# A decoder trunk on one core: S5 local matrices read from memory by overlapping transfers, two K units moved forward, the first block in another order

## The chip, the cores and the metric

One core of one Trainium2 chip. A core has TensorE (PE, matrix products and transposes), VectorE (DVE), ScalarE (ACT), GpSimd (POOL) and SyncE (SP, which issues transfers); each takes its instructions in a written order and waits on semaphores. The metric is the device time of one execution in microseconds (us), median of the runs. "TensorE's pass" below is one matmul instruction.

## The reference

```python
mem_n = _rmsnorm(mem, mem_norm)                       # 256 memory tokens
for i in range(2):                                    # x is (1, 256, 1024)
    g = norm_gains[i]
    x = x + 0.5 * _swiglu(_rmsnorm(x, g[0]), ffn1_w_in[i], ffn1_w_out[i])     # 1024 -> 2 x 2816 -> 1024
    h = _rmsnorm(x, g[1])
    mix = _s5_mixer(h, ...) if i == 0 else _retention_mixer(h, positions, ...)
    x = x + mix
    x = x + _memory_cross_attention(_rmsnorm(x, g[2]), mem_n, w_q[i], w_kv[i], w_o[i])
    x = x + 0.5 * _swiglu(_rmsnorm(x, g[3]), ffn2_w_in[i], ffn2_w_out[i])
return _rmsnorm(x, final_norm)
```

The S5 mixer runs, for each of 64 groups of 16 channels, a diagonal complex state of 64: state = a * state + B u, y = Re(C state) + d * u, then gelu, then a gated product with `w_glu`. The cross attention takes K and V from `mem_n @ w_kv`; they do not depend on x.

## The kernel before

Everything is float32. A product by a weight is made of three matmuls, since a weight tile is split into a rounded part `wh` and a rest `wl`, and the activations likewise (`xTh`, `xTl`): wh by high, wl by high, wh by low. The 256 tokens are two halves of 128 (tt 0 and 1).

**Weight stream** (class `Stream`). A plan, written once, lists all tiles of 512 KB in the order of use. `pump` sends the next load on SP's queue as soon as one of five raw buffers is free (the tile `raw`); ACT makes `wh` (line 86), DVE subtracts to make `wl` (line 88), which frees the raw buffer; seven pairs of `wh`/`wl` exist. Tiles that are tables (fourth field False) are used from the raw buffer itself, and free it only at `ws.done`. SP sends in order: where the next load waits for its buffer, everything behind it on SP waits too. `hold` and `release` put subtractions off and let them go (line 105).

**S5 by chunks of eight steps.** The tokens are regrouped to 32 chunks of 8 steps: after the norm, `S5In.stat(tt)` writes `xn` to memory (`xn_d`) and reads it back in another order (`xc`), half 0 on POOL's queue, half 1 on SP's. `s5` then copies xc to `xg`, transposes it (`U`), multiplies by the V tables (input to state, `v<-...,U`), turns the result to `S`, and runs the scan over 31 chunks on DVE in small steps (`adv`). Beside the scan TensorE makes the part of y that lies inside a chunk: for each of eight q a table of 128 x 1024, the local matrices (a kernel of eight taps, shifted once for each output step), multiplies U. The function `local_table` makes that table: POOL copies the taps into a row of 15 blocks padded by zeros (`pad`), TensorE transposes eight overlapping windows of it, ACT copies the result to `L`. After the scan the C tables (`carry`) add the state's part, then `gelu`, then `y_out` turns y and splits it for the gate product (`yT`). V tables 2 and 3 and C tables 0 to 3 are loaded to tiles of their own (`ytab`, and the unused ends of `kvh`/`kvl`); V and C tables 4 to 7 pass through raw buffers. The tables were computed earlier, by the background list `bg` during the first ffn, and stored by POOL.

**Filler.** Where S5 leaves TensorE idle, `fill(us)` takes steps of the K and V units of layer 0's cross attention: units 0 to 3 are K (8 steps of 6 passes of 256 columns), units 4 and 5 V (8 steps of 6 passes of 512). Layer 1's units are computed after the retention mixer.

**Background list.** `bg_step` runs one yield's worth of `s5_tables` (called `tabs`) or of `mem_steps` (norm and transposes of the memory tokens) at set places of the ffn; `bg_flush` runs what is left, just ahead of the residual add.

**First block.** The order of the first ffn block is written by hand: `turned` transposes x, `high` and `low` make `xTh` and `xTl`, `part(tt, c, ...)` multiplies by weight tile c ("hh" is wh by high, "hl" wl by high, "lh" wh by low), `spin(n)` multiplies a scratch tile n times to keep TensorE running, `next(tabs)` takes a step of the S5 tables, `n0.stat` sums the squares of x on ACT.

## Time and profile before

| | |
|---|---|
| median of 3 runs | 1282.44 us (1281.72 to 1284.2) |
| profiled execution | 1278.4 us, its span 1276.6 us |
| TensorE | busy 1255.8 us (98%), granted clock 0.996 |
| DVE, ACT, POOL | 821.1, 630.0 and 61.4 us |
| memory traffic | 242.05 MB, mean 190 GB/s |

A waits row reads: engine, output, line, what it waited for, total time, times. Busy time of TensorE includes the tails of passes that overlap the next, so the start-to-start distance is the price of a pass. In a windows row the columns are the window, its length, then busy time and count of PE, weight loads, DVE, ACT and POOL, the granted clock, the busy share of the transfer engines, and GB/s.

### The profile page before, as it was taken

The numbers are of one execution on the slowest core, as the hardware profiler recorded it, in microseconds if no ns is written. First come the engines' busy times: TensorE is split into PE (matmuls) and PEld (weight loads), VectorE is DVE, ScalarE is ACT, GpSimd is POOL, SyncE is SP. The second block draws the span as 40 slices with busy tenths as digits, with TensorE's granted clock in tenths as the row PEclk, the third lists the DMA queues.
The fourth block names the chain that finished last, engine by engine and source line by source line (L and its number), as shares of the span: only waits on it lengthen the run. The fifth ranks groups of instructions, "written<-read, shape, count | busy, mean of one in ns | idle before, by whom it ended". The sixth has DMA issues, their size and how long they took to land.

```text
span 1276.6 us, 18149 instructions
## 1 busy us (share of the span) xinstructions
PE 1255.8 (98%) x6884; PEld 1056.3 (83%) x6884; DVE 821.1 (64%) x1142; ACT 630.0 (49%) x849; POOL 61.4 (5%) x116
## 2 busy tenths in 40 slices
PE   8999999898999999999999999999999999999997
PEld 5778888877898888888888888899888898888886
DVE  5989986496667755645655546677665646755543
ACT  5645545455455644444545435544544545644532
POOL 4010001000000000001000000001100000000000
PEclk9999999999999999999999999999999999999999
DMA  7856786655645656664765664653674734766560
GB/s 225 239 182 220 251 272 212 216 199 184 207 155 182 210 181 187 207 189 140 243 190 181 197 191 138 218 186 104 215 233 141 231 103 128 235 198 186 188 188 33
DMA packets 166008, 242.05 MB, mean 190 GB/s; under 512 B 10641, under 2 KB 130049, under 8 KB 165281
## 3 DMA queue, kind: packets, MB, share of 16 engines
q1 hardware_dynamic: 161856, 226.80, 56.4%
q0 software_dynamic: 3552, 13.28, 3.3%
q8 instruction: 54, 0.88, 0.3%
q10 hardware_dynamic: 512, 0.82, 0.2%
q14 instruction: 34, 0.27, 0.1%
HBM read 229.32 MB, written 11.53 MB: 189 GB/s over the span
## 4 chain that ended last, share of the span: by engine, by line
PE 80%; DMA 1%; ACT 1%; issue 0%; DVE 0%; POOL 0%; POOLq 0%; ACTq 0%; DVEq 0%; SPq 0%
PE acc L241 61%; PE kv L241 6%; PE pt L245 4%; PE qk L241 4%; PE q L241 2%; PE s L241 1%; PE o L241 1%; PE y L249 1%; PE rv L241 1%; DMA xn_d<-xn 0%; PE rs L241 0%; DMA raw<-in_xattn_w_kv 0%; DMA xc<-xn_d 0%; PE v L249 0%; ACT yT L328 0%
## 5 line engine op out<-in xcount | busy, mean ns | idle before, releaser
L88 DVE TENSOR_TENSOR wl<-raw,wh 128x1024 fp32r<-128x1024 f32 x404 | 489.3, 1225 | 199.0 <-ACT wh L86 186.9
L86 ACT CAST wh<-raw 128x1024 fp32r<-128x1024 f32 x408 | 423.5, 1051 | 180.7 <-PE acc L241 150.7
L241 PE MATMUL acc<-wh,xTh 128*128 128x512 f32 x864 | 326.3, 398 | 0.2 <-ACT wh L86 0.2
L241 PE MATMUL acc<-wl,xTh 128*128 128x512 f32 x864 | 319.5, 390 | 2.1 <-DVE wl L105 2.1
L241 PE MATMUL acc<-wh,xTl 128*128 128x512 f32 x864 | 320.6, 392 | 0.0
L241 PEld LDWEIGHTS acc<-wl,xTh 128*128 128x128 f32 x864 | 162.5, 188 | 35.2 <-DVE wl L105 2.9
L241 PEld LDWEIGHTS acc<-wh,xTl 128*128 128x128 f32 x864 | 162.3, 188 | 34.8 <-DVE xTl L1342 0.7
L241 PEld LDWEIGHTS acc<-wh,xTh 128*128 128x128 f32 x864 | 162.7, 189 | 34.1 <-ACT wh L86 1.5
L241 PE MATMUL acc<-wh,hTh 128*128 128x512 f32 x352 | 138.7, 394 | 0.0
L241 PE MATMUL acc<-wh,hTl 128*128 128x512 f32 x352 | 137.2, 390 | 0.0
L241 PE MATMUL acc<-wl,hTh 128*128 128x512 f32 x352 | 137.1, 389 | 0.0
L468 ACT ACTIVATE s<-acc,rstd 128x256 f32<-128x256 f32 x88 | 41.8, 474 | 152.0 <-PE acc L241 149.2
L470 DVE SCALAR_TENSOR_TENSOR h<-acc,rstd,s 128x256 f32<-128x256 f32 x88 | 42.3, 480 | 90.9 <-ACT s L468 90.8
L241 PEld LDWEIGHTS acc<-wh,hTl 128*128 128x128 f32 x352 | 66.1, 188 | 14.0
L241 PEld LDWEIGHTS acc<-wh,hTh 128*128 128x128 f32 x352 | 66.1, 188 | 13.9 <-issue 0.6
L241 PEld LDWEIGHTS acc<-wl,hTh 128*128 128x128 f32 x352 | 66.1, 188 | 13.2
L289 ACT ACTIVATE junk<-x 128x512 bf16<-128x512 f32 (+1 forms) x27 | 20.9, 772 | 72.5 <-DVE x L368 70.5
L368 DVE SCALAR_TENSOR_TENSOR x<-acc,x 128x512 f32<-128x512 f32 x28 | 18.5, 686 | 39.1 <-PE acc L241 39.1
L280 POOL TENSOR_SCALAR ms<-ss 128x1 f32<-128x1 f32 x11 | 2.6, 239 | 825.0 <-ACT junk L289 824.9
L241 PE MATMUL acc<-wh,yT 128*128 128x512 f32 x128 | 39.1, 400 | 2.6 <-ACT yT L328 2.4
L241 PE MATMUL acc<-wh,ryT 128*128 128x512 f32 x128 | 40.1, 390 | 0.0
L241 PE MATMUL kv<-memh,wh 128*128 128x256 f32 x128 | 37.0, 289 | 0.0
(297 smaller groups left out, 1611.0 us busy)
## 6 DMA issues: line engine op xcount, KB each, us to landing
raw<-in_ffn_w_in SPq DMA_DIRECT2D x352, 256.0 KB, 4.3
raw<-in_ffn_w_out SPq DMA_DIRECT2D x88, 512.0 KB, 4.3
raw<-in_ret_w_in SPq DMA_DIRECT2D x48, 512.0 KB, 4.4
raw<-in_xattn_w_kv SPq DMA_DIRECT2D x32, 512.0 KB, 4.7
raw<-in_s_w_glu SPq DMA_DIRECT2D x32, 256.0 KB, 4.3
raw<-in_xattn_w_q SPq DMA_DIRECT2D x16, 512.0 KB, 4.9
raw<-in_xattn_w_o SPq DMA_DIRECT2D x16, 512.0 KB, 3.9
raw<-in_ret_w_out SPq DMA_DIRECT2D x16, 512.0 KB, 4.4
```

Source lines behind the costliest of these rows:

```text
L86: self.nc.scalar.copy(hi, raw)
L88: self.nc.vector.tensor_sub(lo, raw, hi.bitcast(F32))
L241: pe.matmul(o, lhsT=a, rhs=b, start=start, stop=stop)
L245: pe.transpose(o, a, i)
L249: pe.matmul(o, lhsT=a, rhs=b, start=start, stop=stop, tile_position=at)
L280: pool.tensor_scalar_add(t, ms, EPS)
L289: act.activation(junk[:, 0:src.shape[-1]], src, AF.Square, scale=1.0 / 32.0, accum_out=ss)
L368: dve.scalar_tensor_tensor(out=o, in0=banks[tt][h], scalar=c, in1=o, op0=ALU.mult, op1=ALU.add)
L468: act.activation(s, bank[:, 0:256], AF.Silu, scale=r)
L470: dve.scalar_tensor_tensor(out=h, in0=bank[:, 256:512], scalar=r, in1=s, op0=ALU.mult, op1=ALU.mult)
```

## The change

- The eight local tables are no longer built on TensorE. In the background list `turn_kernels` transposes the taps of four q at a time (from `pads`) and stores them in a memory tensor `ker_d` of 8 x 240 x 128, whose last 112 rows POOL fills with zeros from a tile `zero`. A table is then one load whose rows overlap (partition p, step t: row p + 16 t): it enters the plan as a stream table through a raw buffer. The steps inside a chunk are now in reversed order in the C tables and in gelu's view.
- The list of K and V units used as filler becomes `early`: layer 0's six units and units 0 and 1 of layer 1. The latter two are stored to `k1_d` by POOL and read back by POOL ahead of layer 1's units, of which four are left.
- Both halves of the regroup go through POOL's queue.
- The fill and scan amounts change (11.8 to 15.8 ahead of the regroup; 2.6 for each table; eight steps kept for the end); six C tables go to tiles of their own, two through raw buffers.
- Ahead of the first carry, the first three gate tiles are fetched with their subtractions held until the first gelu is issued; gelu(1) comes ahead of y_out(0).
- The copies of the C input move from ACT to DVE, with a yield more.
- The first block is in another order, with four warm-up passes more, and four raw buffers in use ahead of the load of the second half of x.

```diff
+EARLY = 2
...
     mem_d = dr.tile([2, P, 2048], F32, tag="mem_d", name="mem_d")
+    k1_d = dr.tile([EARLY, 2, P, 512], F32, tag="k1_d", name="k1_d")
+    ker_d = dr.tile([8, 240, P], F32, tag="ker_d", name="ker_d")
...
     def plan_tab(name, tab, q):
-        plan.append(((name, q), tab[q], (1024,), False))
+        plan.append(((name, q), tab, (1024,) if name != "tabL" else (8, P), False))
...
     plan_ffn(0, 1)
-    for u in range(3):
-        plan_kv(0, u)
+    early = [(0, 0), (0, 1), (0, 2), (1, 0), (0, 3), (0, 4), (0, 5), (1, 1)]
+    for l, u in early[:4]:
+        plan_kv(l, u)
     for q in range(4, 8):
-        plan_tab("tabV", tabV, q)
-    plan_kv(0, 3)
-    plan_kv(0, 4)
-    plan_kv(0, 5)
-    for q in range(4, 8):
-        plan_tab("tabC", tabC, q)
+        plan_tab("tabV", tabV[q], q)
+    plan_kv(*early[4])
+    for q in range(8):
+        k = ker_d[q]
+        plan_tab("tabL", bass.AP(tensor=k.tensor, offset=k.offset, ap=[[P, P], [16 * P, 8], [1, P]]), q)
+        if q == 3:
+            plan_kv(*early[5])
+    for l, u in early[6:]:
+        plan_kv(l, u)
+    for q in range(6, 8):
+        plan_tab("tabC", tabC[q], q)
     plan_in("glu", I["s5_w_glu"][0], D)
...
     plan_rows("ro", I["ret_w_out"][0])
-    for u in range(6):
+    for u in range(EARLY, 6):
         plan_kv(1, u)
...
-    def kv_unit(l, u, mem_t, kv):
+    def kv_unit(l, u, mem_t, kv, store=None):
...
             yield from by_weights(("kv", l, u), mem_t, bank)
-            split(k_view(kv.hi)[:, 2 * u:2 * u + 2], k_view(kv.lo)[:, 2 * u:2 * u + 2], bank)
+            parts = [t[:, 5120:] if store is not None else t[:, 512 * u:512 * u + 512] for t in (kv.hi, kv.lo)]
+            split(*[t.rearrange("p (k m) -> p k m", k=2) for t in parts], bank)
+            if store is not None:
+                for i, t in enumerate(parts):
+                    pool.dma_start(out=store[i], in_=t.bitcast(F32))
         else:
...
         for c in range(2):
-            act.copy(craw[:, c, :, 1], craw[:, c, :, 0])
+            dve.tensor_copy(craw[:, c, :, 1], craw[:, c, :, 0])
+        yield
         Cb = big.tile([P, 2, 32, 2, 16], F32, tag="W1", name="Cb")
...
         s5c["pads"] = pads = [sm.tile([P, 4, 8, 16], F32, tag=t, name="pads", bufs=1) for t in ("sc", "pads")]
-        s5c["pad"] = pad = [sm.tile([P, 15, 16], F32, tag=f"pad{i}", name="pad", bufs=1) for i in range(2)]
-        for i in range(2):
-            pool.memset(pad[i], 0.0)
+        zero = sm.tile([P, P], F32, tag="zero", name="zero", bufs=1)
+        pool.memset(zero, 0.0)
+        pool.dma_start(out=ker_d[:, P:].rearrange("q a x -> a q x"), in_=zero[0:112].unsqueeze(1).to_broadcast([112, 8, P]))
         pwq = pw.rearrange("p c n (j q) -> p c n j q", q=8)
...
             o = sY[:, 1].rearrange("p (c j t h) -> p c j t h", c=2, j=4, t=8)
-            a = [pwq[:, c, 1:9, :, q].rearrange("p n j -> p j n").unsqueeze(3).to_broadcast(full) for c in range(2)]
+            a = [pwq[:, c, 1:9, :, q][:, ::-1].rearrange("p n j -> p j n").unsqueeze(3).to_broadcast(full) for c in range(2)]
             b = [Cq[:, c, :, q].unsqueeze(2).to_broadcast(full) for c in range(2)]
...
             dve.scalar_tensor_tensor(out=pd[:, 7], in0=E16, scalar=dT[:, q:q + 1], in1=pd[:, 7], op0=ALU.mult, op1=ALU.add)
+
+        def turn_kernels(i):
+
+            pt = acc("tp").rearrange("p (q e) -> p q e", q=4)
+            for q in range(4):
+                tr(pt[:, q], pads[i][:, q].rearrange("p s h -> p (s h)"), ident)
+            kt = sm.tile([P, 4, P], F32, tag="kt", name="kt", bufs=1)
+            act.copy(kt, pt)
+            pool.dma_start(out=ker_d[4 * i:4 * i + 4, 0:P].rearrange("q a x -> a q x"), in_=kt)
...
                 yield
+            if q % 4 == 3:
+                turn_kernels(q // 4)
+                yield
...
             dve.scalar_tensor_tensor(out=self.xn[:, tt], in0=x[:, tt, :], scalar=r, in1=self.gb, op0=ALU.mult, op1=ALU.mult)
-            q = (pool, nc.sync)[tt]
+            q = pool
             q.dma_start(out=xn_d[tt].rearrange("j t f -> t j f"), in_=self.xn[:, tt].rearrange("t (j f) -> t j f", j=4))
...
-        L2 = []
...
-        def local_table(q):
-            if not L2:
-                L = big.tile([P, 2, 1024], F32, tag="Yh", name="L2")
-                L2.extend([L[:, 0], L[:, 1]])
-            pd, L = s5c["pad"][q % 2], L2[q % 2]
-            pool.tensor_copy(pd[:, 0:8], s5c["pads"][q // 4][:, q % 4])
-            lv = L.rearrange("p (g t h) -> p t g h", g=8, t=8)
-            for b in range(2):
-                pt = ptb().rearrange("p (t e) -> p t e", t=4)
-                for i in range(4):
-                    t = 4 * b + i
-                    tr(pt[:, i], pd[:, 7 - t:15 - t].rearrange("p s h -> p (s h)"), ident)
-                act.copy(lv[:, 4 * b:4 * b + 4], pt.rearrange("p t (g h) -> p t g h", h=16))
-
-        fill(11.8)
+        fill(15.8)
...
-                    local_table(0)
-                    fill(5.2)
-                    adv(6.1)
-                if q < 7:
-                    local_table(q + 1)
-                fill(1.3)
-                adv(2.6)
-                lv = L2[q % 2].rearrange("p (j g e) -> p j g e", j=4, g=2)
+                    fill(2.6)
+                    adv(2.6)
+                if q == 1:
+                    Y2 = [big.tile([P, 2, 1024], F32, tag=t, name="ytab") for t in ("Yl", "Yh")]
+                    for i, t in enumerate([Y[:, k] for Y in Y2 for k in range(2)] + [t[:, 4096:5120].bitcast(F32) for t in (kv.hi, kv.lo)]):
+                        nc.sync.dma_start(out=t, in_=tabC[i])
+                        tC[i] = t
+                fill(2.6)
+                adv(3.2)
+                lv = tab("tabL", q).rearrange("p (t j g h) -> p j g t h", t=8, j=4, g=2)
...
-                if q == 1:
-                    Y2 = big.tile([P, 2, 1024], F32, tag="Yl", name="ytab")
-                    for i, t in enumerate([Y2[:, 0], Y2[:, 1]] + [t[:, 4096:5120].bitcast(F32) for t in (kv.hi, kv.lo)]):
-                        nc.sync.dma_start(out=t, in_=tabC[i])
-                        tC[i] = t
-        while fill(1.3, keep=2):
+                ws.done(("tabL", q))
+        while fill(1.3, keep=8):
...
             qh, ql = q // 4, q % 4
-            ct = (tC[q] if q < 4 else tab("tabC", q)).rearrange("p (c j e) -> p c j e", c=2, j=4)
+            ct = (tC[q] if q < 6 else tab("tabC", q)).rearrange("p (c j e) -> p c j e", c=2, j=4)
             for c in range(2):
...
                         small(ybank[qh, g][32 * j:32 * j + 32, ql], S[sl, :, (q * 2 + c) * 4 + j], ct[sl, c, j], False, ql == 3 and c == 1, (64 * g, 32 * j))
-            if q >= 4:
+            if q >= 6:
                 ws.done(("tabC", q))
...
             for g in range(2):
-                act.activation(ygv[:, g, 4 * qh:4 * qh + 4], ybank[qh, g].rearrange("p q (t h) -> p q t h", h=16),
+                act.activation(ygv[:, g, 4 * qh:4 * qh + 4], ybank[qh, g].rearrange("p q (t h) -> p q t h", h=16)[:, :, ::-1],
                                AF.Gelu_apprx_tanh)
...
         ws.limit = None
+        ws.hold()
+        ws.get(("glu", 0, 2))
         for q in range(4):
...
         gelu(0)
+        ws.release()
         for q in range(4, 8):
             carry(q)
+        gelu(1)
         y_out(0)
-        gelu(1)
+        fill(2.6)
+        y_out(1)
         fill(99)
-        y_out(1)
         yT = XT(*yT)
...
         act.activation(e, neghalf[:, 0:1], AF.Exp)
-        ws.cap = 3
+        ws.cap = 4
         ws.pump(0)
...
         t0 = turned(x[:, 0, :], gain(0), 0, (0,))
+        spin(2)
         high(t0)
...
         low(t0)
-        spin(2)
+        spin(4)
+        high(t1)
         ws.get((first, 0, 1))
-        high(t1)
+        ws.release(1)
+        part(0, 0, "hh", "lh")
         low(t1)
-        part(0, 0, "hh", "lh")
+        part(0, 1, "hh", "lh")
         ws.release(1)
-        part(0, 1, "hh", "lh")
+        ws.get((first, 0, 2))
         part(0, 0, "hl")
-        ws.get((first, 0, 2))
+        part(0, 1, "hl")
         ws.release(1)
+        ws.get((first, 0, 3))
         part(0, 2, "hh", "lh")
-        part(0, 1, "hl")
+        ws.release(1)
+        part(0, 3, "hh", "lh")
         t0 = turned(x[:, 1, :], gain(0), 1)
         high(t0)
-        ws.release(1)
-        ws.get((first, 0, 3))
+        part(0, 2, "hl")
         low(t0)
-        part(0, 2, "hl")
+        part(0, 3, "hl")
+        for c in range(4):
+            part(1, c, "hh", "hl")
+        ws.release()
         next(tabs)
-        for c in range(3):
-            part(1, c, "hh")
         next(tabs)
-        ws.release()
         n0.stat(0)
-        for c in range(3):
-            part(1, c, "hl")
         next(tabs)
-        part(0, 3, "hh", "lh")
-        for c in range(3):
+        for c in range(4):
             part(1, c, "lh")
-        part(0, 3, "hl")
         n0.stat(1)
-        part(1, 3, "hh", "hl", "lh")
         bg.append(tabs)
...
         def kv0():
-            for u in range(6):
-                for _ in kv_unit(0, u, mem_t[0], kv):
+            for l, u in early:
+                for _ in kv_unit(l, u, mem_t[0], kv, k1_d[u] if l else None):
                     yield 0.65 if u < 4 else 1.3
-        todo = list(range(48))
+        todo = list(range(8 * len(early)))
         g = kv0()
...
+        for u in range(EARLY):
+            for i, t in enumerate((kv.hi, kv.lo)):
+                pool.dma_start(out=t[:, 512 * u:512 * u + 512], in_=k1_d[u, i])
+
         def kv1():
-            for u in range(6):
+            for u in range(EARLY, 6):
                 yield from kv_unit(1, u, mem_t[0], kv)
```

**Place one, SP.** What SP sends from the first `w_kv` tiles up to the C tables (`raw<-ker_d` is a local table, `xn_d` and `xc` the regroup, `ytab`, `kvh` and `kvl<-tabC` the C tables with tiles of their own; 128x4x256 are K tiles, 128x2x512 V tiles). Before:

```order
L68 DMA raw<-in_xattn_w_kv 128x4x256 x5
L805 DMA ytab<-tabV 128x1024 x2
L68 DMA raw<-in_xattn_w_kv 128x4x256
L68 DMA raw<-tabV 128x1024 x3
L811 DMA xn_d<-xn 128x4x256
L814 DMA xc<-xn_d 64x2048
L68 DMA raw<-tabV 128x1024
L68 DMA raw<-in_xattn_w_kv 128x4x256 x2
L68 DMA raw<-in_xattn_w_kv 128x2x512 x8
L68 DMA raw<-tabC 128x1024 x4
L921 DMA ytab<-tabC 128x1024 x2
```

After:

```order
L69 DMA raw<-in_xattn_w_kv 128x4x256 x5
L831 DMA ytab<-tabV 128x1024 x2
L69 DMA raw<-in_xattn_w_kv 128x4x256 x3
L69 DMA raw<-tabV 128x1024 x4
L69 DMA raw<-in_xattn_w_kv 128x4x256 x2
L69 DMA raw<-ker_d 128x8x128 x4
L69 DMA raw<-in_xattn_w_kv 128x2x512 x3
L922 DMA ytab<-tabC 128x1024 x4
L922 DMA kvh<-tabC 128x1024
L922 DMA kvl<-tabC 128x1024
L69 DMA raw<-in_xattn_w_kv 128x2x512
L69 DMA raw<-ker_d 128x8x128 x4
```

The two regroup transfers are gone from SP; four table loads stand ahead of the V tiles of unit (0,4), six C tables ahead of its last tile, and the last four tables behind that.

**Place two, POOL.** The norms of the two halves and the regroup, up to what follows. Before:

```order
L280 TENSOR_SCALAR ms<-ss 128x1
L283 TENSOR_TENSOR rstd<-ms,neghalf 128x1
L811 DMA xn_d<-xn 128x4x256
L814 DMA xc<-xn_d 64x2048
L282 TENSOR_SCALAR ms<-ss 128x1
L283 TENSOR_TENSOR rstd<-ms,neghalf 128x1
L835 COPY pad<-pads 128x128 x8
```

After:

```order
L289 TENSOR_SCALAR ms<-ss 128x1
L292 TENSOR_TENSOR rstd<-ms,neghalf 128x1
L837 DMA xn_d<-xn 128x4x256
L840 DMA xc<-xn_d 64x2048
L291 TENSOR_SCALAR ms<-ss 128x1
L292 TENSOR_TENSOR rstd<-ms,neghalf 128x1
L837 DMA xn_d<-xn 128x4x256
L840 DMA xc<-xn_d 64x2048
L568 DMA k_d<-kvh 128x512
L568 DMA k_d<-kvl 128x512
```

Half 1's two transfers follow its norm on POOL, the copies of the taps are gone, and the stores of the first of layer 1's K units come behind.

**Place three, TensorE in the first block.** From the transposes of half 1 of x on (`lam` and `e` belong to the S5 tables' first steps). Before:

```order
L241 MATMUL acc<-wl,xTh 128x512 x2
L245 MATMUL pt<-ident,x 128x128 x8
L241 MATMUL acc<-wl,xTh 128x512 x2
L245 MATMUL pt<-ident,lam 128x32 x2
L245 MATMUL pt<-ident,e_224 128x32
L241 MATMUL acc<-wh,xTh 128x512 x6
L241 MATMUL acc<-wl,xTh 128x512 x6
L241 MATMUL acc<-wh,xTh 128x512 x2
L241 MATMUL acc<-wh,xTl 128x512 x8
L241 MATMUL acc<-wl,xTh 128x512 x2
```

After:

```order
L254 MATMUL pt<-ident,x 128x128 x8
L250 MATMUL acc<-wl,xTh 128x512 x4
L250 MATMUL acc<-wh,xTh 128x512 x2
L250 MATMUL acc<-wl,xTh 128x512 x2
L250 MATMUL acc<-wh,xTh 128x512 x2
L250 MATMUL acc<-wl,xTh 128x512 x2
L250 MATMUL acc<-wh,xTh 128x512 x2
L250 MATMUL acc<-wl,xTh 128x512 x2
L250 MATMUL acc<-wh,xTh 128x512 x2
L250 MATMUL acc<-wl,xTh 128x512 x2
L254 MATMUL pt<-ident,lam 128x32 x2
L254 MATMUL pt<-ident,e_253 128x32
```

The transposes of `lam` and `e` stood two passes behind those of x; now 20 passes stand between.

On TensorE the memory transposes move too: four groups of four (`mem_raw`) stood six passes apart, and 48 passes followed the last up to the first filler pass; now the last two groups are one run of eight, put there by the flush, and 36 passes follow it.

## The prediction

> **What bounds the kernel now.** I read the page's busy times, then the waits of TensorE, then the S5 stretch (190 to 312 us) engine by engine, and last its transfers. The page:
>
> ```profile
> PE 1255.8 (98%) x6884; PEld 1056.3 (83%) x6884; DVE 821.1 (64%) x1142; ACT 630.0 (49%) x849; POOL 61.4 (5%) x116
> ...
> L88 DVE TENSOR_TENSOR wl<-raw,wh 128x1024 fp32r<-128x1024 f32 x404 | 489.3, 1225 | 199.0 <-ACT wh L86 186.9
> L86 ACT CAST wh<-raw 128x1024 fp32r<-128x1024 f32 x408 | 423.5, 1051 | 180.7 <-PE acc L241 150.7
> ```
>
> TensorE is the bound: it works 1255.8 of 1276.6 us. A cast of a weight tile costs ACT 1.05 us and the subtraction behind it costs DVE 1.22. So an edit can gain only what it takes off TensorE, or out of these waits (engine, what it waited for, total, times, longest):
>
> ```profile
> PE pt L245 <- ACT xg L848: 3.5, 1, 3.5
> PE acc L241 <- ACT yT L328: 2.4, 1, 2.4
> PE acc L241 <- DVE wl L105: 2.1, 1, 2.1
> ...
> PE y L249 <- issue: 0.9, 1, 0.9
> ...
> PE tp L245 <- ACT craw L696: 0.3, 1, 0.3
> ```
>
> The third is in the first block; the first, second and fourth are in S5. The profiled execution took 1278.4 us, 4.0 under the median of the runs shown (1282.44). I sum against 1278.4 and move the result by 4.0.
>
> **Transposes out, two turns in.** Prices, from the groups of the S5 stretch, the timeline of TensorE and the chain of waits:
>
> ```profile
> L245 PE MATMUL pt<-ident,pad 128*128 128x128 f32 x64 | 8.8, 279 | 0.2 <-ACT S L876 0.2
> L842 ACT COPY L<-pt 128x512 f32<-128x512 f32 x16 | 8.7, 591 | 9.4 <-PE pt L245 9.4
> 222.38 0.28 PE L241 MATMUL kv<-memh,wh 128*128 128x256 f32 x1
> 222.50 0.28 PE L241 MATMUL kv<-meml,wh 128*128 128x256 f32 x1
> 259.33 1.39 PE kv L241 x6
> ```
>
> The 64 transposes of the padded kernels show 8.8 us, but the last of each eight overlaps what follows by most of its 0.28, so 8.8 − 8 × 0.25 = 6.8 us leave TensorE. The 16 copies (8.7 us of ACT) go too; TensorE waited for none of them, so they count nothing. The two new groups of four transposes cost 4 × 0.11 = 0.45 each, 0.9 in all. Net **−5.9**. The copies of C move to DVE with a yield between: **−0.3**, the whole craw wait.
>
> **Two K units moved.** A K step is six matmuls 0.12 apart, 0.72 us, and a unit has eight: 5.76 us. The later stage from which two units go is full:
>
> ```profile
> 978.00:1026.00 48.00, 48.00 (x308) 43.82 (x307) 32.38 (x35) 26.80 (x34) 0.88 (x2) 1.00 0.68 216
> ```
>
> (The second number is TensorE's busy time in the 48 us.) It gives back 11.5 us there, and S5 pays 11.5: six steps (4.3 us) ahead of the regroup, ten steps (7.2) behind it. Moving them is **0** unless they fill idle time, and that is counted with the waits. Their way through memory (POOL writes, then POOL reads at the layer's start) ends at most some 9 us after the issue (the slowest POOL row below), with four K/V units still to compute before anything reads it: 0.
>
> **Memory steps pushed back.** Three new yields in the background list push the last two groups of memory transposes to the flush just ahead of the residual add of token half 0. DVE takes the groups and then the add:
>
> ```profile
> 204.00 0.69 DVE L314 TENSOR_TENSOR t<-pt,gT 128x512 f32<-128x512 f32 x1 [2.14 <-PE pt L245]
> ...
> 206.06 0.68 DVE L314 TENSOR_TENSOR t<-pt,gT 128x512 f32<-128x512 f32 x1
> ...
> 211.99 1.28 DVE L368 SCALAR_TENSOR_TENSOR x<-acc,x 128x512 f32<-128x512 f32 x2
> 215.47 1.28 DVE L809 SCALAR_TENSOR_TENSOR xn<-x,rstd,gb 128x1024 f32<-128x1024 f32 x1 [2.19 <-POOL rstd L283]
> 216.67 4.63 DVE L88 TENSOR_TENSOR wl<-raw,wh 128x1024 fp32r<-128x1024 f32 x4
> 221.21 1.28 DVE L368 SCALAR_TENSOR_TENSOR x<-acc,x 128x512 f32<-128x512 f32 x2
> 224.57 1.29 DVE L809 SCALAR_TENSOR_TENSOR xn<-x,rstd,gb 128x1024 f32<-128x1024 f32 x1 [2.08 <-POOL rstd L283]
> ```
>
> A group takes 206.06 − 204.00 = 2.06 us. Now eight transposes (0.9) stand where half 0 ends (Q), so the add starts at Q + 0.9 + 4.1 = Q + 5.0 instead of Q; xn starts 3.5 later and takes 1.2, and the first of the four subtractions ends 1.2 after that, at Q + 10.9. TensorE has 36 matmuls of half 1 left (8.2 us), so its first filler, which needs that subtraction at once, is due at Q + 9.1 plus two matmuls. Before, the subtraction ended at 217.9 and the filler began at 220.23, 2.3 us of cover; now **+1.4** of waiting (0 to 2).
>
> **Regroup on POOL.** The half-1 add is still behind four subtractions, so xn of half 1 ends about 9.8 us after the due start K of the filler; before, 5.6 (225.86 − 220.23). Its transfers, from the timelines of POOL and TensorE, the chain of waits, and the table of DMA issues:
>
> ```profile
> 217.05 0.85 POOL L811 DMA_DIRECT2D xn_d<-xn  x1 [1.62 <-DVE xn L809]
> 221.84 0.54 POOL L814 DMA_DIRECT2D xc<-xn_d  x1 [3.94 <-DMA xn_d<-xn]
> 225.89 6.06 DMA xn_d<-xn
> 232.04 4.70 DMA xc<-xn_d
> xc<-xn_d POOLq DMA_DIRECT2D x1, 512.0 KB, 8.6
> 237.58 1.09 PE L245 MATMUL pt<-ident,xg 128*128 128x128 f32 x8 [3.52 <-ACT xg L848]
> ```
>
> On POOL the store took 4.8 from issue to the next issue, on SP 6.1; the load back took 4.7 (SP, with the queue empty) or 8.6 (POOL, beside weight loads). SP no longer stands waiting for half 1, so it sends four loads into that time, and the 8.6 is nearer than before. Landing: K + 9.9 + 4.8 + 4.7 to 8.6 = K + 19.4 to 23.3, and 0.8 of copying (236.74 to 237.58). TensorE arrives at K + 1.4 + 25 × 0.72 = K + 19.4. The wait is 0.8 to 4.7; the copies may queue behind a cast, so I take 3.0 against 3.5 now: **−0.5** (−2.7 to +1.5). The six extra steps are eaten by the 4.2 us by which the row of half 1 is late. The Trainium skill ("DMA: Bandwidth & Descriptors", on issuing engines not being separate DMA queues) says that queues of different engines share the same sixteen DMA engines, so that only issue time is saved. The 8.6 against 4.7 agrees with it.
>
> **Raw buffers.** The tables now pass through the five raw weight buffers, and four of them are loaded far ahead. V weight tiles are left with what is freed tile by tile. Rates (a window's last number is GB/s) and landings:
>
> ```profile
> 271.00:277.00 6.00, 6.00 (x63) 4.54 (x62) 5.55 (x29) 2.19 (x5) 0.44 (x1) 1.00 1.00 400
> raw<-in_ffn_w_out SPq DMA_DIRECT2D x88, 512.0 KB, 4.3
> kvl<-tabC SPq DMA_DIRECT2D x1, 512.0 KB, 8.2
> 246.58 0.39 PE L241 MATMUL kv<-memh,wh 128*128 128x256 f32 x1
> ...
> 250.78 1.21 PE L245 MATMUL pt<-ident,pad 128*128 128x128 f32 x8 [0.21 <-ACT S L876]
> ```
>
> Let V = 0 stand at 246.58, where the v stage ends. TensorE then runs to 4.2 as before, ten K steps to 11.4, y(0) (0.6) to 12.0, a K step and tile c0's two V steps (2.8) to 15.5, y(1) to 16.1, and so on, 3.4 us for each tile and table. Unit (0,4): c0's load waits for the last K subtraction, near 4.5; landing 4.3, cast, subtraction: 11.1. Then c1's load: ready near 17.5, due 16.3: wait 1.2. c2 is sent after y(0), at 12.0, with six C tables right behind it, and c3 after y(1): 8 × 0.524 MB at 400 GB/s is 10.5 us, and 4.3 − 1.3 of fixed time: c3 lands near 25.4 and is cast and subtracted by 27.7; due at 24.3 (with the 1.2): wait 2.8 after cast and subtraction overlap. Unit (0,5) c0 is sent when c3 is subtracted and follows four table loads; with 4.3 to 5.5 of landing it is ready near 34 and due at 30.5: 3.2. The later tiles fit. Together **+7.2**; the ends are 0 (everything a little earlier) and 14 (half the rate).
>
> The 512-byte runs of the overlapping tables are shorter than any bulk load here. The Trainium skill (the same page, Specifications) gives 512 bytes as the smallest transfer at line rate, which speaks against the half rate; no run here shows it. That table also gives about 358 GB/s per core from memory; the window's 400 is above it, so the row is used, and by 358 the sum would be 1.2 more.
>
> **Carry and gelu.** ACT now casts three gate weight tiles before the first gelu, and the third's load waits for the last K unit. TensorE then waits about 4.4 for the first y_out, where now four waits add to 3.9 (0.9, two near 0.3, 2.4); the eight K steps kept cover the rest. **+0.5** (−2.4 to +4).
>
> **First block.** TensorE, DVE and ACT:
>
> ```profile
> 6.81 1.06 PE L241 MATMUL warm<-warm 128*128 128x512 bf16 x2
> 17.85 0.73 PE L241 MATMUL acc<-wl,xTh 128*128 128x512 f32 x2 [2.08 <-DVE wl L105]
> 19.18 0.24 PE L245 MATMUL pt<-ident,e 32*128 32x32 f32 x1 [0.36 <-DVE e L594]
> 26.29 0.39 PE L241 MATMUL acc<-wh,xTh 128*128 128x512 f32 x1
> 22.44 1.98 ACT L86 CAST wh<-raw 128x1024 fp32r<-128x1024 f32 x2
> 23.50 2.36 DVE L88 TENSOR_TENSOR wl<-raw,wh 128x1024 fp32r<-128x1024 f32 x2 [2.06 <-ACT wh L86]
> ```
>
> The 2.1 us wait goes: other work stands there. But the e transpose moves behind 16 more matmuls (3.7 us), and ACT works in order: its exponentials and sums follow e, then the casts of the second block, 22.44 − 19.18 = 3.3 after e. Wait and lower clock gone, e comes near 21.1; casts from 24.4, first subtraction done at 26.6; TensorE, which has 8 matmuls left after e, waits for it and starts block two at about 26.3, as now. Two more warm-up matmuls (0.43 each) ahead of the first real one are within that. **0** (−2.1 to +2).
>
> **Sum.** −5.9 − 0.3 + 0 + 1.4 − 0.5 + 7.2 + 0.5 = +2.4: 1280.8 for a profiled execution, 1284.8 beside the median. This is hardly outside 0.2% (2.6 us), about what a measurement of this kernel can tell from no change.
>
> **Rivals.** (a) It does what it says: loads run a little earlier and no V tile is late, xg lands in time, the 2.1 goes. Then −5.9 − 0.3 − 2.1 + 0 − 2.7 + 0 + 0.5 = −10.5, and with some 2 of waits left −8.5: 1274. For it: 98% busy means small covers suffice, and 7.2 of extra filler stand behind the regroup. Against: the filler needs weights through the same five buffers. Chance 0.32. (b) The other side: the overlapping reads run at half rate, every table holds the transfer engines 1.3 us longer, and the waits for V tiles go from 7.2 to 14; +9.2: 1291.6. It decides once a table takes over 2 us of all engines. Chance 0.25. (c) My sum, gains eaten by V-tile waits, −0.5 to +6: 0.43. That the change doesn't do what it says can't be for the transposes: they are gone; it can be for the regroup, which is in (c).
>
> **Numbers.** Range 1270 to 1296: from 2 below the best sum of (a) to 4 above (b), past which some 2 in 10 are left (a slower rate yet, or a late xg on top); the likeliest case alone is 1282 to 1288. Faster: (a) and a little of (c), 0.34. Within 0.2%: half of (c), 0.22. Slower: 0.44.
>
> **What would show it.** No row of transposes of pads; waits of TensorE for wh or wl of w_kv tiles at the y tables, in sum near 7; a wait for wl at the first filler near 1.4; the xg wait still near 3; the stage of the later K/V units 11.5 shorter; block two starting near 26.3. If the V-tile waits sum to under 2, (a) holds and I am some 6 too high; if the table loads land later than 7 us, (b).

## The result and the profile after

The changed kernel takes 1303.03 us (median of 4 runs, 1301.68 to 1306.59) against 1283.07 for the kernel before: a ratio of 1.0165 with a 95% interval of 1.0151 to 1.0179. It is slower by 20 us, past the upper end of the forecast (1296). The profiled execution took 1306.6 us, 3.6 above its median, where that of before lay 4.7 below its own; so the two traces differ by 28.2 us of span, and some 8 of that is the spread of executions.

The stages tell where. Their bounds are the first filler matmul, the end of the v stage, and the first matmul of the gate product. Windows of the kernel before:

```profile
0.00:220.23 220.23, 214.81 (x1090) 170.56 (x1091) 185.31 (x291) 116.64 (x166) 33.08 (x55) 1.00 0.72 227
220.23:246.58 26.35, 22.59 (x271) 21.82 (x270) 11.27 (x14) 9.09 (x16) 2.90 (x5) 0.94 0.66 205
246.58:300.25 53.67, 51.86 (x647) 42.19 (x643) 41.57 (x141) 28.66 (x41) 3.46 (x6) 1.00 0.60 201
300.25:1276.60 976.35, 966.53 (x4885) 821.76 (x4883) 582.95 (x697) 475.61 (x628) 21.93 (x50) 1.00 0.57 180
```

and of the changed kernel, between the same places of the program:

```profile
0.00:227.33 227.33, 219.01 (x1102) 173.05 (x1103) 182.32 (x289) 115.48 (x164) 31.06 (x56) 0.98 0.71 222
227.33:263.38 36.05, 27.89 (x308) 26.44 (x306) 17.99 (x21) 13.62 (x22) 3.66 (x6) 0.91 0.61 191
263.38:344.40 81.02, 61.65 (x643) 50.05 (x639) 51.65 (x151) 29.60 (x34) 1.12 (x2) 0.85 0.77 241
344.40:1304.80 960.40, 953.08 (x4788) 809.54 (x4786) 569.91 (x685) 465.02 (x615) 25.11 (x56) 1.00 0.57 179
```

The lengths differ by +7, +10, +27 and −16. The last is the two K units (11.5) and before's wait in the gate product (2.4, with a slow clock behind it). In the third stage TensorE is idle for 81.0 − 61.6 = 19.4 us instead of 1.8, and is busy for 9.8 us more with work that differs by 0.4 only (7.2 of filler in, 6.8 of transposes out): the clock column says why, 0.85 instead of 1.00. TensorE's waits in the changed kernel:

```profile
PE y L258 <- DVE S L897: 7.7, 1, 7.7
PE pt L254 <- ACT xg L859: 6.5, 1, 6.5
PE kv L250 <- DVE wl L89: 3.7, 4, 1.4
PE kv L250 <- DVE S L897: 3.0, 1, 3.0
PE acc L250 <- ACT wh L87: 3.0, 3, 2.0
PE kv L250 <- ACT wh L87: 2.9, 2, 1.5
PE tp L254 <- DVE craw L709: 2.7, 1, 2.7
```

Two rows need care. Of the 3.7 for `wl`, 1.45 stand at the first filler, which is a K tile. And the 3.0 that the profile puts to the scan (`kv <- S`) belong to a matmul that reads no S:

```profile
299.95 1.04 ACT L87 CAST wh<-raw 128x1024 fp32r<-128x1024 f32 x1 [1.90 <-DMA raw<-in_xattn_w_kv]
...
301.05 0.50 PE L250 MATMUL kv<-wh,memh 128*128 128x512 f32 x1 [3.04 <-DVE S L897]
```

The cast that makes its `wh` ends at 300.99, and in the run with half 1 on SP (below) the same matmul waits 3.1, there put to `wh`. So the V tiles (the other `kv <- wl` and `kv <- wh` rows) make TensorE wait 2.9 + 2.3 + 3.0 = 8.2 us, near the forecast (7.2), and the scan 7.7, which was not in the sum. SP's queue, ACT and DVE show how the one makes the other:

```profile
279.77 0.39 SPq L69 DMA_DIRECT2D raw<-in_xattn_w_kv  x1
282.06 10.31 SPq L69 DMA_DIRECT2D raw<-ker_d  x4
293.18 15.67 SPq L69 DMA_DIRECT2D raw<-in_xattn_w_kv  x6
...
290.85 1.04 ACT L87 CAST wh<-raw 128x1024 fp32r<-128x1024 f32 x1 [8.59 <-DMA raw<-in_xattn_w_kv]
...
291.92 1.23 DVE L89 TENSOR_TENSOR wl<-raw,wh 128x1024 fp32r<-128x1024 f32 x1 [4.26 <-ACT wh L87]
```

Tile c3, the last of V unit (0,4), is sent at 279.77, behind six C tables, lands 11.1 us later, and DVE stands for 4.26 us at its subtraction with scan steps behind it. Over the whole scan DVE stands 13.9 us at such subtractions. The next V tile is not sent before that subtraction, at 293.18. Such waits are then paid a second time. TensorE's timeline at tile c1, where two waits follow each other:

```profile
280.83 0.50 PE L250 MATMUL kv<-wh,memh 128*128 128x512 f32 x1 [1.48 <-ACT wh L87]
282.09 0.50 PE L250 MATMUL kv<-wl,memh 128*128 128x512 f32 x1 [0.76 <-DVE wl L89]
...
283.09 0.63 PE L250 MATMUL kv<-wl,memh 128*128 128x512 f32 x1
283.51 0.63 PE L250 MATMUL kv<-wh,meml 128*128 128x512 f32 x1
...
287.76 0.40 PE L250 MATMUL kv<-wh,memh 128*128 128x512 f32 x1
288.00 0.39 PE L250 MATMUL kv<-wl,memh 128*128 128x512 f32 x1
```

The starts are 0.42 apart after the waits and 0.24 some 4.5 us later. The Trainium skill ("TensorE: Matmul & The Clock Gate", Part 1) says that an idle TensorE falls to half its clock and needs sustained work of about 3.4 us to come back; these rows agree with the half rate, which lasts here from 282.66 to 286.07. It puts the idle time at about 3.4 us too; here 2.2 us in two pieces were enough.

### The profile page after: what moved, and what is told of

It reads as the page before. It is cut to its first block, busy times and chain, and to the rows that moved or that the text cites. A ratio compares the mean times of both kernels' runs of the same rounds, so it can differ in the third digit from the quotient of the medians.

```text
span 1304.8 us, 18035 instructions
## 1 busy us (share of the span) xinstructions
PE 1261.6 (97%) x6832; PEld 1059.1 (81%) x6832; DVE 821.9 (63%) x1144; ACT 623.7 (48%) x833; POOL 60.9 (5%) x120
## 4 chain that ended last, share of the span: by engine, by line
PE 75%; DMA 4%; DVE 2%; ACT 1%; issue 1%; SPq 0%; POOL 0%; POOLq 0%; DVEq 0%; ACTq 0%
PE acc L250 60%; PE qk L250 4%; PE kv L250 3%; DMA raw<-in_xattn_w_kv 3%; PE pt L254 3%; PE q L250 2%; DVE wl L89 1%; PE s L250 1%; PE o L250 1%; PE rv L250 1%; DMA raw<-in_s_w_glu 0%; PE rs L250 0%; ACT wh L87 0%; PE v L258 0%; DVE yT L338 0%
## 5 line engine op out<-in xcount | busy, mean ns | idle before, releaser
L87 ACT CAST wh<-raw 128x1024 fp32r<-128x1024 f32 x408 | 423.6, 1051 | 225.2 <-PE acc L250 151.3
L250 PE MATMUL acc<-wh,xTh 128*128 128x512 f32 x864 | 327.5, 399 | 3.1 <-ACT wh L87 3.0
L250 PE MATMUL acc<-wl,xTh 128*128 128x512 f32 x864 | 321.4, 392 | 1.3 <-DVE wl L89 1.0
L250 PE MATMUL acc<-wh,xTl 128*128 128x512 f32 x864 | 321.6, 393 | 0.0
L250 PEld LDWEIGHTS acc<-wh,xTh 128*128 128x128 f32 x864 | 162.9, 189 | 37.7 <-ACT wh L87 4.8
L250 PEld LDWEIGHTS acc<-wl,xTh 128*128 128x128 f32 x864 | 163.3, 189 | 34.6 <-DVE wl L89 2.1
L250 PEld LDWEIGHTS acc<-wh,xTl 128*128 128x128 f32 x864 | 162.7, 189 | 34.7 <-DVE xTl L1355 0.3
L250 PE MATMUL acc<-wh,hTh 128*128 128x512 f32 x352 | 139.1, 395 | 0.0
L250 PE MATMUL acc<-wh,hTl 128*128 128x512 f32 x352 | 137.3, 390 | 0.0
L250 PE MATMUL acc<-wl,hTh 128*128 128x512 f32 x352 | 137.2, 390 | 0.0
L250 PEld LDWEIGHTS acc<-wh,hTh 128*128 128x128 f32 x352 | 66.1, 188 | 13.9 <-issue 0.8
L250 PEld LDWEIGHTS acc<-wh,hTl 128*128 128x128 f32 x352 | 66.1, 188 | 14.0
L250 PEld LDWEIGHTS acc<-wl,hTh 128*128 128x128 f32 x352 | 66.2, 188 | 13.2
L250 PE MATMUL acc<-wh,ryT 128*128 128x512 f32 x128 | 40.1, 391 | 0.0
L250 PE MATMUL kv<-memh,wl 128*128 128x256 f32 x128 | 37.1, 290 | 1.4 <-DVE wl L89 1.4
L250 PE MATMUL kv<-memh,wh 128*128 128x256 f32 x128 | 37.9, 296 | 0.0
```

The lines of the kernel that those rows point to most:

```text
L87: self.nc.scalar.copy(hi, raw)
L250: pe.matmul(o, lhsT=a, rhs=b, start=start, stop=stop)
```

## The experiments

The ratio stands against the kernel before, with its 95% interval. By these intervals, a difference of less than some 3 us between two variants of the changed kernel can't be told from none.

**Is it the table loads?** Seven of the eight loads left out of the changed kernel, so that one table serves all eight q:

```diff
     for q in range(8):
         k = ker_d[q]
+        if q == 0:
             plan_tab("tabL", ...)
-                lv = tab("tabL", q)...
+                lv = tab("tabL", 0)...
```

> Leaves out seven of the eight table loads: one local table stays in one raw buffer and serves all eight q. Theory S (tables take the raw buffers, V tiles come late, the scan behind their subtractions too): no TensorE wait for V tiles or S, V stage to gate product some 22 to 27 us shorter, 1276 to 1283 us. Rival R (the overlapping 512-byte reads are slow) expects the same here. Rival C (the loss is elsewhere: first block, craw, regroup): less than 8 us off, above 1295.

1299.41 us, 1.0140 (1.0123 to 1.0158): 3 us back, not 20, and those at the edge of the noise. The theory in that form fell. But the waits had changed: none for V tiles in place of 8.2, and a new one, `PE kv L251 <- DVE kvl L339: 11.6`. ACT stood for 8.78 us at the cast of the next tile in the plan, a K tile sent behind the six C tables, and the copy that frees a PSUM bank stood behind it.

**Is it the short overlapping reads?** The same loads from contiguous rows (those of the C tables, so as many bytes of other values):

```diff
-        plan_tab("tabL", bass.AP(... [[P, P], [16 * P, 8], [1, P]]), q)
+        plan_tab("tabL", tabC[q].rearrange("p (t x) -> p t x", t=8), q)
```

> The eight tables are read as contiguous 4 KB rows (of the C tables, so the values are others), same bytes, same buffers. Theory S: no change, 1300 to 1305 us, same waits. Rival R: the waits for V tiles shrink by half or more, below 1296.

1302.31 us, 1.0161 (1.0143 to 1.0179): no change, and the V tiles make TensorE wait 8.2 as before. Rival (b), in which a slower rate makes these waits, is out. Median landing of the tables in the changed kernel, and of the ten loads that the same group holds here:

```profile
raw<-ker_d SPq DMA_DIRECT2D x8, 512.0 KB, 7.1
```

```profile
raw<-tabC SPq DMA_DIRECT2D x10, 512.0 KB, 5.6
```

The overlapping reads do hold the transfer engines longer. Windows of 70 us around the eight tables, of the changed kernel and of this one, move the same bytes at a busy share of 0.71 and 0.63, which makes 5.6 us, or 0.7 a table (an estimate from these two rows):

```profile
250.00:320.00 70.00, 55.06 (x474) 43.11 (x474) 39.67 (x127) 21.00 (x27) 1.12 (x2) 0.88 0.71 223
```

```profile
248.50:318.50 70.00, 55.04 (x474) 43.10 (x474) 39.74 (x127) 21.02 (x27) 1.13 (x2) 0.85 0.63 223
```

**Is it the scan?** Only the first two of its 30 steps, the rest left out:

```diff
-            for n in range(2, 32):
+            for n in range(2, 4):
```

> Leaves out 28 of the 30 scan steps. Theory S: the waits for S (10.7 us) and the slow clock behind them go, the waits for V tiles (some 6.6) stay: 1286 to 1293 us. Rival T (the scan's own length holds the subtractions of V tiles up): these waits go too, below 1284.

1296.99 us, 1.0119 (1.0104 to 1.0135). The S wait is gone (7.7), but the waits for V tiles went from 8.2 to 10.0, and 6 us came back. So the tiles are late without the scan too. That the scan is late by the tiles rests on DVE's 13.9 us above; its own length has a part in it, since 2.2 us of S wait stay in the last run with one table below, where no V tile is late.

**More buffers?**

```diff
-RAW_BUFS = 5
-W_BUFS = 7
+RAW_BUFS = 7
+W_BUFS = 6
```

> Seven raw buffers and six wh/wl pairs instead of five and seven. Theory S: two more buffers let V tiles be sent earlier; half or more of the waits for V tiles and S go: 1284 to 1295 us. Rival R: the transfers are as slow, at most 4 us off.

1311.43 us, 1.0237 (1.0215 to 1.0258). The waits for V tiles are gone, so two more buffers do bring the first unit's tiles in time. But the first tile of the next unit is now sent behind ten tables, ACT stands 17.36 us at its cast, and TensorE waits 12.1 (`kv <- kvl`). From the turn of vc to the gate product it is 71.8 us instead of 79.5, but six pairs cost elsewhere: `PE acc L250 <- ACT wh L87: 15.5, 9, 2.6`. For the time this run is not clean, since it takes a pair away.

**Is it the burst of C tables, or the order on ACT and DVE?** One C table for each y table from 1 to 6; and, apart from it, the planner told of the transfers, with the scan steps ahead of the filler (lines abridged):

```diff
-                if q == 1:            # six tables at once
+                if 1 <= q <= 6:       # spread: table q - 1
...
+                    ws.other(9.0)                   # other_adv
-            ws.other((3.0, 6.0)[tt])
+            ws.other((3.0, 14.0)[tt])
-                fill(2.6); adv(3.2)
+                adv(3.2); fill(2.6)
```

> The six C tables with tiles of their own are sent one at each of the y tables 1 to 6 instead of all six at y table 1. Leaving out seven local tables gained some 3 us only, so the raw buffers are not the whole cause. Theory B (the burst of six holds the next V tile's load up by 8 us, and DVE's scan stands behind that tile's subtraction): the c3 landing falls from 11 to about 5 us, the wait for S by half; 8 to 14 us off, 1289 to 1295. Rival O (the loads are late anyhow; it is the order of ACT and DVE that hands the lateness on): within 4 us of 1303.

> The planner is told of the late transfers (9 us for the six C tables, 14 instead of 6 for half 1's regroup), and at each y table the scan steps are written ahead of the filler, so that fewer casts and subtractions stand in front of xg and of the scan. Loads are as in the changed kernel. Theory O: the waits for xg and S fall from 6.5 and 10.7 to under 5 and 4, 8 to 14 us off. Theory B: the waits move to the V tiles, at most 4 us off.

1300.25 us, 1.0144 (1.0125 to 1.0164), and 1305.99 us, 1.0185 (1.0163 to 1.0206). Neither theory alone, and neither time clear of the changed kernel's. In the first c3 lands 4.6 us after it is sent, as expected of it, but the S wait stays at 7.9. In the second the xg wait fell to 4.4 and the S wait to 5.2, and TensorE waited 10.4 for V tiles and 6.2 for gelu's output instead. Its trace also parts the xg wait. In the changed kernel xg's copies stand behind a cast that waits for its tile; here they wait for the regroup's own load:

```profile
251.65 1.04 ACT L87 CAST wh<-raw 128x1024 fp32r<-128x1024 f32 x1 [10.30 <-DMA raw<-in_xattn_w_kv]
...
253.07 1.14 ACT L859 COPY xg<-xc 128x512 f32<-128x512 f32 x2
```

```profile
249.51 1.14 ACT L859 COPY xg<-xc 128x512 f32<-128x512 f32 x2 [3.85 <-DMA xc<-xn_d]
```

So of the 6.5 us some 2.1 are the cast and 4.4 the late load.

**One table, the C tables spread and the planner told, together** (1.5 us told for each C table; the filler stays ahead of the scan steps):

> One local table for all eight q (seven loads left out), the six C tables one at a time, and the planner told of them and of half 1's regroup. Each of the three alone gave at most 4 us and passed the wait on to the next late thing. Theory P (late loads meet ACT's and DVE's fixed order at three places in a row, so all must go): the waits for kvl and S go, 1280 to 1290 us. If it stays above 1295, the V tiles are late for another reason, such as the filler's place alone.

1291.80 us, 1.0075 (1.0052 to 1.0098): 11 us back where the parts gave 3, 3 and −3. The losses stand in a row, and what is taken out at one place comes up at the next.

**The edits ahead of it.** The memory steps as before (C's copies on ACT, no extra yields); half 1 on SP; the first block as before; and e 18 passes earlier in the new first block:

```diff
-            dve.tensor_copy(craw[:, c, :, 1], craw[:, c, :, 0])    # no_yields
-        yield
+            act.copy(craw[:, c, :, 1], craw[:, c, :, 0])
                 turn_kernels(q // 4)
-                yield
-            q = pool                                               # half1_sp
+            q = (pool, nc.sync)[tt]
         low(t0)                                                    # e_early
+        next(tabs)
+        next(tabs)
         part(0, 3, "hl")
```

> C's copies on ACT as before and none of the three extra yields, so that the memory steps stand where they stood. If the delay of the memory steps and the copy on DVE cost what the trace shows (2.7 us and some 3.5 of slow clock behind it, 1.4 at the first filler, 3 of the xg wait): 6 to 10 us off, 1293 to 1297. If the xg wait only comes from transfers: 4 to 6 off.

> Half 1 of the regroup on SP again. SP stands still for it, so its load back shares with nothing (4.7 instead of 8.0 us) but the next K tile comes later. If the regroup's transfers set the xg wait: 6.5 falls to 3 to 4 and 2 to 5 us come off. If the K tile's cast in front of xg sets it: no change or some 2 us slower.

> The changed kernel with the first block (and three raw buffers ahead of x's second half) as before. By the trace the new order saved 2.1 us of waiting, then lost 2.8 waiting for the second block's casts and some 1.6 to slow clock: 1 to 3 us off, 1300 to 1302. If the new order is worth its place: 1 to 2 us slower.

> The changed kernel with the transposes of lam and e 18 passes earlier, so that ACT comes to the second block's casts 3 to 4 us earlier. If ACT's order behind e makes the second block late: the 2.8 us wait and the slow clock behind it go, 3 to 5 us off, 1298 to 1300. If it is DVE's or the loads' order: under 1 us.

The memory steps: 1297.19 us, 1.0122 (1.0100 to 1.0143), 5.8 us back, just under what was expected. The xg wait falls only from 6.5 to 4.5; the wait at the first filler (1.45) is gone, and that for the copy of C falls from 2.7 to 0.3. In the changed kernel the latter and the spacing behind it read

```profile
68.32 1.11 PE L254 MATMUL tp<-ident,craw 128*128 128x128 f32 x4 [2.69 <-DVE craw L709]
...
70.09 0.63 PE L250 MATMUL acc<-wh,xTl 128*128 128x512 f32 x1
70.52 0.63 PE L250 MATMUL acc<-wh,xTh 128*128 128x512 f32 x1
```

0.43 apart up to 74.4. On ACT the copies had cost 0.3.

Half 1 on SP: 1303.98 us, 1.0174 (1.0156 to 1.0191), no change; the xg wait is 8.2, with a cast ahead of xg's copies that waits 11.90 for its tile. While that cast stands there, the queue cannot show. First block as before: 1301.38 us, 1.0158 (1.0139 to 1.0177), not to be told from no change; e earlier: 1299.21 us, 1.0140 (1.0121 to 1.0159), 3.2 us back by the ratios, at the edge of the noise; in its trace the second block starts at 24.05 without a wait.

**Parts alone on the kernel before.** Only the two K units, with the fill amounts that belong to them; then the same with `ws.other((3.0, 14.0)[tt])`:

> The kernel before (tables turned on TensorE, regroup on SP and POOL, first block as it was) with only the two K units of layer 1 as filler, 15.8 of filler ahead of the regroup and eight steps kept for the end. If the extra filler by itself is sound, it fills the 3.5 us xg wait and part of the 2.4 us yT wait: 1276 to 1281 us. If its loads crowd out the V tiles as in the changed kernel: 1284 or more.

> The kernel before with the two K units, and the planner told that half 1's regroup takes 14 us, so that the K tile's cast stands behind xg's copies on ACT and not ahead. If that cast, which waits 10.7 us for its load, makes the xg wait of 7.0: it falls to 3 to 4 and 3 to 5 us come off, 1281 to 1284. If the regroup's own transfers are late: at most 1 us off.

1286.74 us, 1.0045 (1.0030 to 1.0060), and 1279.52 us, 0.9987 (0.9977 to 0.9998). The first has six steps (4.3 us) more of cover and twice the xg wait; the second has next to none:

```profile
PE pt L247 <- ACT xg L854: 7.0, 1, 7.0
```

```profile
PE pt L247 <- ACT xg L854: 0.5, 1, 0.5
```

Between them only that number differs: in the first the K tile's cast stands ahead of xg's copies,

```profile
244.07 1.04 ACT L87 CAST wh<-raw 128x1024 fp32r<-128x1024 f32 x1 [10.71 <-DMA raw<-in_xattn_w_kv]
```

and waits 10.7 us for its load; in the second it stands behind them. Here, with half 1 on SP, the cause of the xg wait is shown. With half 1 on POOL and the planner told 4.4 were left, in another kernel; whether the queue makes that difference was not run.

**Only the tables on the kernel before** (no K units; first block, C's copies, memory steps, regroup and gate tiles as before), and the same with seven loads left out:

> The kernel before with only the local tables through memory (and the C tables and fill amounts that go with them): no K units, first block, C's copies, memory steps, regroup and gate tiles as before. If the tables by themselves starve the V tiles and the scan: y stage 10 us or more longer, 1288 to 1296. If they only hurt together with the K units and the late transfers in front of them: within 3 us of the kernel before or up to 6 faster (the transposes gone).

> The run with only the local tables through memory (1304.1), with seven of the eight loads left out and one table serving all q. If the loads, by the raw buffers that they hold, cost the 22 us: the waits for V tiles, S and yg go, 1276 to 1284. If the fill and C-table amounts that came with the tables cost them: above 1295.

1304.06 us, 1.0175 (1.0157 to 1.0192), and 1282.96 us, 1.0015 (1.0003 to 1.0027). So the tables by themselves cost what the whole change costs, and it is the loads: seven fewer give 21 us back. Whether by the buffers that they hold or by the time of the transfers, this pair of runs does not tell. Their waits, with the loads and without:

```profile
PE kv L249 <- ACT wh L87: 8.9, 3, 5.4
PE pt L253 <- ACT yg L962: 6.1, 1, 6.1
PE y L257 <- DVE S L894: 5.8, 1, 5.8
PE kv L249 <- DVE wl L89: 4.2, 6, 0.8
```

```profile
PE pt L254 <- ACT yg L964: 6.5, 2, 6.3
...
PE y L258 <- DVE S L895: 2.2, 1, 2.2
```

The waits for V tiles (13.1) are gone. In the stretch with the loads the clock is 0.83:

```profile
247.00:331.00 84.00, 58.90 (x663) 44.18 (x656) 48.33 (x148) 26.82 (x33) 0.00 (x0) 0.83 0.72 224
```

Even without the loads, and with 56 transposes left out, it is no faster than before: the yg wait is 6.5. In its trace the second gelu stands on ACT behind three casts of gate tiles, whose loads went out after the C tables; that these tables and the fill amounts make the wait was not tried apart.

**Repairs, and a better kernel.** The changed kernel with e earlier (behind part(1, 0)), C's copies on ACT, no extra yields, spread C tables and the planner told; and the kernel before with the first block in that order; and both parts that gained:

> The changed kernel (all eight tables loaded) with four repairs: C's copies on ACT and no extra yields, e earlier in the first block, the C tables one at a time, the planner told of them and of half 1. If the losses of the parts add: 1303 less 5.8, 3, 3 and 2 to 4, 1287 to 1290. If the starvation by the tables rules whatever is repaired around it: above 1292.

> The kernel before with the first block in the changed order but the transposes of lam and e 12 passes earlier. If the new order is good and only e's place spoils it: the 2.1 us wait goes and nothing comes in its place, 1278 to 1281 where the kernel before has 1282. If the second block is bound by ACT's casts anyway: no change.

> The kernel before with both parts that gained: the two K units with half 1's regroup told to the planner (ratio 0.9987), and the new first block with e earlier (0.9980). If they add: 0.9967, 1276 to 1279 us, faster than both kernels. If the K units only moved a wait that the first block's gain runs into: 1280 to 1282.

The repaired one takes 1294.83 us, 1.0102 (1.0084 to 1.0121): with all eight loads the V tiles still make TensorE wait 10.6. The first block on the kernel before: 1279.18 us, 0.9980 (0.9969 to 0.9991), faster than both kernels. With the K units added: 1278.98 us, 0.9980 (0.9971 to 0.9989), no more than that alone; the two gains (0.20% and 0.13%) did not add, and why was not tried further.

## Why the prediction was wrong

The sign was right; the sum was +2.4 and the profiles show +28 (medians +20). Stage by stage, the terms gave +0.6, +5.2, +8.1 and −11.5 where +7, +10, +27 and −16 were measured.

- **Raw buffers (+7.2): the step that failed.** Its mechanism held. c3 was said to land near V + 25.4, and is cast at 290.85, V + 27.5 (V is 263.38 there); the next unit's c0 was said to be ready near V + 34, and is subtracted at 302.26, V + 38.9. The three waits for V tiles were put at 1.2, 2.8 and 3.2 and measured 2.2, 2.2 and 3.8: 8.2 for 7.2. The words "the later tiles fit" and the sum stopped at these waits. What also stands behind a late tile was left out: the scan on DVE (7.7 us of waits), and the slow clock after waits (9.4 us in the stage, its extra busy time less the 0.4 of work). Range and rival (b) took the 7 to 14 by a slower rate. By its own sign (landings later than 7 us) rival (b) would hold, as the median is 7.1; contiguous rows showed that the rate is not the cause.
- **Regroup (−0.5): wrong in sign.** It took a wait of 3.0 out of 0.8 to 4.7, and 6.5 was measured. The load alone came at the late end (4.4), and "the copies may queue behind a cast", priced at a few tenths, added some 2.1. In the kernel before with the K units, where half 1 is on SP, moving that cast took a wait of 7.0 to 0.5.
- **Memory steps (+1.4)** measured 1.45 at the first filler. **C's copies (−0.3)** were wrong in sign: on DVE the copies stand behind three subtractions of weight tiles, and TensorE waited 2.7 us for them, with a slow stretch behind it.
- **First block (0).** The 2.1 us wait went (with no lower clock behind it in the kernel before, 1.00 from 18 to 24 us), and e came at 20.45 (forecast 21.1, with 16 passes more ahead of it where 18 are). TensorE took up the second block with waits of 2.03 and 0.77 and met its first wl matmul at 26.03, as forecast; then it ran at 0.43 for 3.5 us. Undone, it is no different; with e earlier it gains.
- **Transposes (−5.9) and K units (0)** hold as amounts of work. Rival (a), nothing late, is refuted by its own sign: 8.2 of waits for V tiles where it needs under 2.

## What to carry to other kernels

A load that is late costs its wait on each engine that reads in order: price what stands behind the waiting cast and the waiting subtraction, not only the matmul that needs the tile, and add the slow clock that can follow a wait of TensorE. When work is turned from an engine to transfers, count the buffers that the transfers hold and the loads that then stand behind them, not their rate alone: seven of the eight loads through the stream's buffers cost 21 us, where all the transposes that the tables replace cost 6.8. A planner that places casts by assumed landings must be told of every transfer that it does not send itself; on the kernel before with the K units one number (14 instead of 6) was worth 7 us.

## What the runs showed that was not expected

TensorE's clock was halved after single waits of 2.69, 2.36 and 2.24 us (for the copy of C, in the changed kernel, with contiguous rows and with one table) and after two of 1.48 and 0.76, and came back after 3 to 6 us of work. At the first block a wait of 2.1 us left it at 1.00 in the kernel before, and was followed by 0.50 in the run with only the tables. So a wait of 2 to 3 us can cost about twice its length, and does not always. Overlapping reads with runs of 512 bytes land in 7.1 us against 5.6 for contiguous rows and hold the transfer engines some 0.7 us longer a table (the estimate above), and the kernel's time is the same. The Trainium skill ("DMA: Bandwidth & Descriptors", Specifications) puts the smallest transfer at line rate at 512 bytes. The kernel's time agrees; the busy share of 0.71 against 0.63 for the same bytes does not.
